# Three stacked blocks on one core: the experts' low weight parts all on VectorE, the embeddings' product at the routing, the last gate's weights as blocks of the experts' pipeline

## The chip, the cores and the metric

The kernel runs on one core of one Trainium2 chip. The metric is the time of one execution on the device in microseconds; the time before is the median of three runs. All sums below are made on one profiled execution of the kernel before.

## The reference, cut to what matters

Three blocks follow each other on 512 tokens of 1024 numbers: an mLSTM and sparse attention block, a gated recurrent and gMLP block, and a block with 32 experts. The change touches only the end of the third. There a router picks 4 of 32 experts for each token, each expert is a gated product with 1024 x 2048 weights and a second one with 1024 x 1024, and the rows are added up per token. Then come a layer norm, a gate of the embeddings `p` and a last layer norm:

```python
def third_block(x, p, ...):
    ...
    x = layer_norm(DEEPNORM_ALPHA_3 * x + mix, ln1_g[i], ln1_b[i])
    ffn = moe(x, router_w[i], router_b[i], w_gate_up[i], b_gate_up[i], w_down[i], b_down[i])
    x = layer_norm(DEEPNORM_ALPHA_3 * x + ffn, ln2_g[i], ln2_b[i])
    gate = jax.nn.sigmoid((x @ ple_gate_w[i] + ple_gate_b[i]).astype(jnp.float32)).astype(x.dtype)
    ple = p[i] @ ple_proj[i]
    x = layer_norm(DEEPNORM_ALPHA_3 * x + gate * ple, ln3_g[i], ln3_b[i])
```

The product `ple` needs nothing of `x`, so it may be made at any time. All numbers are float32.

## The kernel before, in words

A float32 product is made of three products of shorter floats (`mm3`): the weights are split into a high part `hi`, which ScalarE (ACT) writes as a rounded copy, and a low part `lo`, which is the difference of the weights and `hi`. So each block of weights goes through three rings of tiles of 1 MB each: `wl` (where it lands), `wh` (high) and `wo` (low). In the experts' stage `wl` has 5 tiles and `wh` and `wo` have 4 each.

The experts' stage is `run`. Its list `steps` has 384 entries of one 1 MB block each: expert i has 8 `wide` steps (`w_gate_up`, 12 matmuls each), and behind them stand 4 `narrow` steps (`w_down`, 12 matmuls each) of expert i-1. In each step `load` issues the transfer of a block 7 steps ahead on SyncE's queue (SP), `halve` makes the two parts of the block 3 steps ahead, and `step` runs the matmuls. In `halve` ACT makes `hi`, and `lo` is subtracted by VectorE (DVE) in three steps of four and by GpSimd (POOL) in every fourth (`n % 4 == 1`). POOL also gathers the tokens of the expert after next (`fetch`, tile `xg`) and adds the finished rows to `yd` in memory (`add_rows`). DVE also makes the gated activation (`glu`) and the low parts of the tokens (`turn`). Each engine runs its instructions in the order in which they are written; within the experts' steps that is the program's order (`manual_schedule`), elsewhere a scheduler sets it.

Ahead of the experts' steps the routing works token tile by token tile (`route`, `places`, `biased`): layer norm, transposes, logits, the choice of four, the positions. Behind them `ple` and `ended` do the end: `project` makes the product of the embeddings with `ple_proj` (8 transposes, 48 matmuls into `pa`), four blocks of `ple_gate_w` are loaded and split, the rows of `yd` come back as `zs`, are normed, turned and multiplied with the gate's weights (`pz`), and are normed once more.

In PSUM the tag `gemm` has 4 banks, and `run` calls `layout` so that `aux` and `hold` have 2 each.

Of the kernel before, what the change touches and what calls it, by code (L numbers as in the profile page):

```python
# [19 lines left out]
P = 128  # L20
S = 512
D = 1024
# [8 lines left out]

class Env:
    def __init__(self, ctx, tc):
        self.tc, self.nc = tc, tc.nc
        nc = self.nc
        self.n = 0
# [4 lines left out]
        self.psx = ctx.enter_context(ExitStack())  # L41
        self.layout(gemm=4, aux=3, hold=1)
        self.dram = ctx.enter_context(tc.tile_pool(name="dr", bufs=1, space=bass.MemoryType.DRAM))
        self.ident = self.cst.tile([P, P], F32, name="ident")
        make_identity(nc, self.ident)
        self.half = self.cst.tile([P, 1], F32, name="half")
        nc.gpsimd.memset(self.half, -0.5)
        self.rings = {"wl": [(self.wl, "wl")] * 3, "wh": [(self.wh, "wh")] * 2, "wo": [(self.wo, "wo")] * 2}
        self.at = dict.fromkeys(self.rings, 0)
        self.banks, self.owner = [], {}  # L50
# [20 lines left out]
    def name(self, s):  # L71
        self.n += 1
        return f"{s}_{self.n}"

    def layout(self, **banks):

        self.BANKS = banks
        self.psx.close()
        self.psp = self.psx.enter_context(self.tc.tile_pool(name=self.name("ps"), bufs=4, space=bass.MemoryType.PSUM))

# [1266 lines left out]
class Moe:  # L1347
# [58 lines left out]

    def project(self, pj, lp):

        e, nc, a = self.e, self.e.nc, self.a
        parts = lp.tile([P, 2, 2, 4, P], F32R, tag="xp", name="parts", bufs=3).rearrange("p g a k n -> p (g a) (k n)")  # L1410
        hi, lo = parts[:, :2, :], parts[:, 2:, :]
        for t in range(NT):
            pt = self.wp.tile([P, 512], F32, tag="g", name=e.name("pt"))[:, :256]
            nc.sync.dma_start(pt, a["p_3"][0, 0, t * P:(t + 1) * P, :])
            pz = e.ps("pz").rearrange("p (a b) -> p a b", a=4)
            for j in range(2):
                nc.tensor.transpose(pz[:, j, :], pt[:, j * P:(j + 1) * P], e.ident)
            ts = slice(t * P, (t + 1) * P)
            e.split(hi[:, :, ts], lo[:, :, ts], pz[:, :2, :])

        def got(t, c, n, pz):
            nc.scalar.activation(pj[t][:, c:c + n], pz, AF.Copy)
        e.gemm_tok([(hi, lo)], 2, a["ple_proj_3"][0], 0, D, got)
# [117 lines left out]
    def run(self, out):  # L1541
        e, nc, tc, wp = self.e, self.e.nc, self.e.tc, self.wp
        e.layout(gemm=4, aux=2, hold=2)
        ph = ExitStack()
# [64 lines left out]
        for i in range(N_EXP + 1):  # L1609
# [6 lines left out]
        lands, tiles = [], []  # L1616

        def load(n):
            if n < len(steps):
                land = e.ring("wl")  # L1620
                nc.sync.dma_start(land.rearrange("p a b -> p (a b)"), steps[n][3])
# [18 lines left out]
        with tc.manual_schedule():  # L1640
# [23 lines left out]
        ph.close()  # L1664
        self.ple(out)

# [110 lines left out]

    def ple(self, out):

        with self.e.tc.tile_pool(name=self.e.name("pl"), bufs=1) as lp:  # L1780
            self.ended(out, lp)

    def ended(self, out, lp):
        e, nc, a, wp = self.e, self.e.nc, self.a, self.wp
        wg, w, rows = a["ple_gate_w_3"][0], {}, []

        def row_pair(land, nm):
# [3 lines left out]
        land = e.res.tile([P, NT, D], F32, tag="res", name="rows")  # L1791
        own = lp.tile([P, 6, D], F32, name="own")
        zs, pj = [own[:, t, :] for t in range(NT)], [own[:, 4, :], own[:, 5, :]] + [land[:, 2 + i, :] for i in range(2)]
# [9 lines left out]
        def first(t):  # L1803
            z = zs[t]
            nc.sync.dma_start(z, self.yd[t * P:(t + 1) * P, :])
            if t == 0:
                for k0 in (0, 4):
                    w[512, k0] = e.wblock(wg, k0, 4, 512, 512, z[:, 0:1], ("wl", "wl") if k0 else ("wh", "wo"))
            if t == 1:
                nc.vector.tensor_copy(land[:, 0:2, 0], z[:, 0:2])  # L1810
                row_pair(land, "ln3")
            norm(z, 0)
# [3 lines left out]
        def gate(t):  # L1816
            z = zs[t]
            for c in (0, 512):
# [8 lines left out]
                nc.scalar.activation(g, pz, AF.Sigmoid)  # L1827
                nc.vector.tensor_tensor(g, g, pj[t][:, cs], op=ALU.mult)
                nc.vector.scalar_tensor_tensor(z[:, cs], z[:, cs], ALPHA, g, op0=ALU.mult, op1=ALU.add)
# [6 lines left out]
        for t in range(NT):  # L1836
# [3 lines left out]
            if t:  # L1840
                last(t - 1)
        last(NT - 1)


# [48 lines left out]
```

## Time and profile before

| | us |
|---|---|
| time before, median of 3 runs (3303.92 to 3329.73) | 3324.47 |
| the profiled execution's own time | 3329.63 |
| its span | 3327.9 |
| stretch before the routing of the last tiles, 0 to 1881 | 1881 |
| routing, 1881 to 1944 | 63 |
| experts' steps, 1944 to 3244 | 1300 |
| end, 3244 to 3328 | 84 |

Times in the rows are counted from the start of the span. "PE" is TensorE, "PEld" its loading of weights. A matmul's end is modelled, so two starts that follow each other tell its cost better than its duration. What stands in brackets behind a row is how long the engine was idle before it, and what ended that.

### The profile page before, as it was taken

The numbers are of one execution on the slowest core, as the hardware profiler recorded it, in microseconds if no ns is written. First come the engines' busy times: TensorE is split into PE (matmuls) and PEld (weight loads), VectorE is DVE, ScalarE is ACT, GpSimd is POOL, SyncE is SP. The second block draws the span as 40 slices with busy tenths as digits, with TensorE's granted clock in tenths as the row PEclk, the third lists the DMA queues.
The fourth block names the chain that finished last, engine by engine and source line by source line (L and its number), as shares of the span: only waits on it lengthen the run. The fifth ranks groups of instructions, "written<-read, shape, count | busy, mean of one in ns | idle before, by whom it ended". The sixth has DMA issues, their size and how long they took to land. (4 is left out here: it accounts for less than half of the span.)

```text
span 3327.9 us, 36769 instructions
## 1 busy us (share of the span) xinstructions
PE 3157.5 (95%) x14603; PEld 2392.9 (72%) x14603; DVE 2246.5 (68%) x2365; ACT 1518.3 (46%) x1547; POOL 905.0 (27%) x333
## 2 busy tenths in 40 slices
PE   7999999999999999999999989999999999989987
PEld 6776877878777787888778766666666666666666
DVE  5853687444726533722345769899898898899876
ACT  5353333323635223122313246666666666666652
POOL 2310011101000001100000125555555555555531
PEclk9997999999999999999999979999999999999999
DMA  4212465333121423222223269899998999898882
GB/s 141 77 39 81 145 206 197 108 114 102 51 76 51 124 89 134 94 89 89 94 93 105 107 244 342 326 335 333 341 340 323 329 337 331 325 330 325 323 301 98
DMA packets 180207, 639.50 MB, mean 192 GB/s; under 512 B 25656, under 2 KB 33184, under 8 KB 130810
## 3 DMA queue, kind: packets, MB, share of 16 engines
q1 hardware_dynamic: 172858, 611.89, 51.0%
q0 software_dynamic: 7168, 25.17, 3.2%
q8 instruction: 117, 1.92, 0.2%
q14 instruction: 64, 0.52, 0.0%
HBM read 616.01 MB, written 21.01 MB: 191 GB/s over the span
## 5 line engine op out<-in xcount | busy, mean ns | idle before, releaser
L1629 DVE TENSOR_TENSOR wo<-wl,wh 128x2048 fp32r<-128x2048 f32 x288 | 945.6, 3309 | 129.1 <-ACT wh L1627 125.3
L1627 ACT ACTIVATE wh<-wl 128x2048 fp32r<-128x2048 f32 x384 | 725.2, 1912 | 164.0 <-PE pgu L167 104.3
L99 DVE TENSOR_TENSOR wo<-wl,wh 128x2048 fp32r<-128x2048 f32 (+2 forms) x147 | 320.9, 2186 | 543.3 <-ACT wh L98 534.6
L1629 POOL TENSOR_TENSOR wo<-wl,wh 128x2048 fp32r<-128x2048 f32 x96 | 486.8, 5071 | 531.0 <-ACT wh L1627 521.3
L167 PE MATMUL pf<-ah,wo 128*128 128x512 f32 (+1 forms) x1520 | 564.2, 371 | 1.2 <-DVE wo L99 1.2
L166 PE MATMUL pf<-ah,wh 128*128 128x512 f32 (+1 forms) x1520 | 563.3, 371 | 0.6 <-ACT wh L98 0.6
L98 ACT ACTIVATE wh<-wl 128x2048 fp32r<-128x2048 f32 (+2 forms) x153 | 277.5, 1817 | 621.1 <-PE pf L168 320.9
L168 PE MATMUL pf<-al,wh 128*128 128x512 f32 (+1 forms) x1520 | 560.0, 369 | 0.0
L168 PE MATMUL pgu<-wo,xe 128*96 128x512 f32 x1024 | 413.9, 404 | 47.9 <-DVE wo L1629 47.9
L166 PE MATMUL pgu<-wh,xe 128*96 128x512 f32 x1024 | 416.9, 407 | 0.0
L167 PE MATMUL pgu<-wh,xe 128*96 128x512 f32 x1024 | 412.1, 402 | 0.0
L166 PEld LDWEIGHTS pf<-ah,wh 128*128 128x128 f32 x1520 | 287.4, 189 | 58.8 <-ACT cy L728 6.9
L168 PEld LDWEIGHTS pf<-al,wh 128*128 128x128 f32 x1520 | 286.5, 189 | 51.7 <-issue 3.7
L167 PEld LDWEIGHTS pf<-ah,wo 128*128 128x128 f32 x1520 | 287.2, 189 | 49.5 <-DVE wo L99 1.4
L168 PEld LDWEIGHTS pgu<-wo,xe 128*96 128x96 f32 x1024 | 170.3, 166 | 129.8 <-DVE wo L1629 57.2
L168 PE MATMUL pd<-wo,h 128*96 128x512 f32 x512 | 207.1, 405 | 37.4 <-DVE wo L1629 36.7
L167 PEld LDWEIGHTS pgu<-wh,xe 128*96 128x96 f32 x1024 | 170.0, 166 | 68.1 <-issue 1.2
L166 PEld LDWEIGHTS pgu<-wh,xe 128*96 128x96 f32 x1024 | 170.1, 166 | 66.3 <-issue 0.9
L167 PE MATMUL pd<-wh,h 128*96 128x512 f32 x512 | 205.3, 401 | 4.1 <-DVE h L114 4.1
L166 PE MATMUL pd<-wh,h 128*96 128x512 f32 x512 | 205.6, 402 | 2.0 <-ACT h L113 1.1
L168 PEld LDWEIGHTS pd<-wo,h 128*96 128x96 f32 x512 | 84.7, 165 | 87.2 <-DVE wo L1629 51.1
L1561 POOL DMA_INDIRECT xg<-x3d,src x32 | 126.4, 3948 | 72.8 <-DVE src L1559 54.7
(476 smaller groups left out, 4615.8 us busy)
## 6 DMA issues: line engine op xcount, KB each, us to landing
wl<-w_gate_up SPq DMA_DIRECT2D x256, 1024.0 KB
wl<-w_down SPq DMA_DIRECT2D x138, 1024.0 KB
wl<-w_in SPq DMA_DIRECT2D x54, 1024.0 KB
wl<-w_ada SPq DMA_DIRECT2D x24, 1024.0 KB
wl<-w_up SPq DMA_DIRECT2D x20, 1024.0 KB
wl<-w_ffn_in SPq DMA_DIRECT2D x20, 1024.0 KB
wl<-w_out SPq DMA_DIRECT2D x12, 1024.0 KB
wl<-w_ffn_out SPq DMA_DIRECT2D x10, 1024.0 KB
```

The costliest lines, as they stand in the source:

```text
L98: nc.scalar.activation(hi[:, :nk, :n], land[:, :nk, :n], AF.Copy)
L99: (eng or nc.vector).tensor_tensor(lo[:, :nk, :n], land[:, :nk, :n], hi[:, :nk, :n].bitcast(F32), op=ALU.subtract)
L166: mm(out, st[0], mv[0], start=first, stop=False)
L167: mm(out, st[1], mv[0], start=False, stop=False)
L168: mm(out, st[0], mv[1], start=False, stop=last)
L1561: nc.gpsimd.indirect_dma_start(out=rows[i], out_offset=None, in_=self.xd, in_offset=bass.IndirectOffsetOnAxis(ap=src[:, :1], axis=0))
L1627: nc.scalar.activation(hi, land, AF.Copy)
L1629: eng.tensor_tensor(lo, land, hi.bitcast(F32), op=ALU.subtract)
```

## The change

- `halve`: DVE subtracts `lo` in all steps; POOL subtracts none.
- `project` is called at the start of `run`, so it stands in the program at the routing. Its result is kept in a tile `pj` of 16 KB per partition, its split embeddings take a tile of the `wh` ring, and the 48 matmuls, 8 transposes and 6 transfers move with it.
- The four blocks of `ple_gate_w` are four more entries of `steps`, without matmuls: they are loaded and halved like an expert's, and their tiles are kept for the end.
- `layout` is gone: `aux` has 3 banks and `hold` 1 throughout, and an expert's second accumulator `pd` comes from `aux`. The rows of the last two layer norms are both loaded into `wl`, `y` has one buffer, and the rows `zs` have a pool of their own.

```diff
-        self.layout(gemm=4, aux=3, hold=1)
+    BANKS = {"gemm": 4, "aux": 3, "hold": 1}
...
     def run(self, out):
-        e.layout(gemm=4, aux=2, hold=2)
+        self.project()
...
-                acc[i] = [e.ps("pd", "hold")[:CAP, :] for _ in range(2)]
+                acc[i] = [e.ps("pd", tag)[:CAP, :] for tag in ("hold", "aux")]
...
-            y = wp.tile([P, D], F32, tag="y", name=e.name("y"))[:CAP, :]
+            y = wp.tile([P, D], F32, tag="y", name=e.name("y"), bufs=1)[:CAP, :]
...
+        wg = self.a["ple_gate_w_3"][0]
+        steps += [(None, c, k0, wg[k0 * P:(k0 + 4) * P, c:c + 512].rearrange("(k p) n -> p k n", p=P)) for c in (0, 512) for k0 in (0, 4)]
...
                 nc.scalar.activation(hi, land, AF.Copy)
-                eng = nc.gpsimd if n % 4 == 1 else nc.vector
-                eng.tensor_tensor(lo, land, hi.bitcast(F32), op=ALU.subtract)
+                nc.vector.tensor_tensor(lo, land, hi.bitcast(F32), op=ALU.subtract)
...
                 halve(n + ahead)
+                if step is None:
+                    w[i, k] = tiles.pop(0)
+                    continue
...
-        self.ple(out)
+        self.ple(out, w)
...
-        self.project(pj, lp)
-        row_pair(e.ring("wl").rearrange("p (g i) n -> p g (i n)", g=2), "ln2")
-        for k0 in (0, 4):
-            w[0, k0] = e.wblock(wg, k0, 4, 0, 512)
...
-            if t == 0:
-                for k0 in (0, 4):
-                    w[512, k0] = e.wblock(wg, k0, 4, 512, 512, z[:, 0:1], ("wl", "wl") if k0 else ("wh", "wo"))
```

How the order changes is shown at three places. The first is SP's queue at the routing, before the change: `w_gate_up` is an expert's weights, `x3d` and `yd` are the tokens written to memory, of which the last `x3d` waits for the last tile's layer norm.

```order
L1621 DMA wl_13236<-w_gate_up 128x2048
L1621 DMA wl_13238<-w_gate_up 128x2048
L1429 DMA x3d<-xres 128x1024 x2
L1776 DMA yd<-xres 128x1024
L1429 DMA x3d<-xres 128x1024
L1621 DMA wl_13240<-w_gate_up 128x2048
L1776 DMA yd<-xres 128x1024
L1621 DMA wl_13242<-w_gate_up 128x2048
L1621 DMA wl_13244<-w_gate_up 128x2048
L1621 DMA wl_13250<-w_gate_up 128x2048
L1429 DMA x3d<-xres 128x1024
```

The same queue after the change, where `ple_proj` and `p` are the embeddings' weights and rows.

```order
L88 DMA wl_13167<-ple_proj 128x2x512
L88 DMA wl_13205<-ple_proj 128x2x512
L1425 DMA x3d<-xres 128x1024 x2
L1776 DMA yd<-xres 128x1024
L1425 DMA x3d<-xres 128x1024
L1776 DMA yd<-xres 128x1024
L1410 DMA pt_13139<-p 128x256
L1410 DMA pt_13146<-p 128x256
L1425 DMA x3d<-xres 128x1024
L1619 DMA wl_13338<-w_gate_up 128x2048
L1410 DMA pt_13153<-p 128x256
L1410 DMA pt_13160<-p 128x256
```

Six loads of experts' weights stood ahead of the last `x3d`; now none does, and the second of them stands behind the last rows of `p`.

The second place is DVE between an expert's gated activation `g` and the low parts of `h`, before the change.

```order
L1534 SCALAR_TENSOR_TENSOR g_20032<-u_20038,g_20032 96x512
L1629 TENSOR_TENSOR wo_20045<-wl_19942,wh_20044 128x2048
L1629 TENSOR_TENSOR wo_20065<-wl_19968,wh_20064 128x2048
L1629 TENSOR_TENSOR wo_20101<-wl_20012,wh_20100 128x2048
L114 SCALAR_TENSOR_TENSOR h_20120<-pt_20121,h_20120 128x384
L114 SCALAR_TENSOR_TENSOR h_20128<-pt_20129,h_20128 128x384
```

The same after the change.

```order
L1530 SCALAR_TENSOR_TENSOR g_20134<-u_20140,g_20134 96x512
L1626 TENSOR_TENSOR wo_20147<-wl_20044,wh_20146 128x2048
L1626 TENSOR_TENSOR wo_20167<-wl_20070,wh_20166 128x2048
L1626 TENSOR_TENSOR wo_20185<-wl_20096,wh_20184 128x2048
L1626 TENSOR_TENSOR wo_20203<-wl_20114,wh_20202 128x2048
L109 SCALAR_TENSOR_TENSOR h_20222<-pt_20223,h_20222 128x384
L109 SCALAR_TENSOR_TENSOR h_20230<-pt_20231,h_20230 128x384
```

All four subtractions stand on DVE where three did; TensorE's order in the experts' steps is the same before and after.

The third place is SP's queue at the end, before the change, from the last expert's weights on.

```order
L1621 DMA wl_22312<-w_down 128x2048
L1414 DMA pt_22466<-p 128x256
L1414 DMA pt_22473<-p 128x256
L93 DMA wl_22494<-ple_proj 128x2x512
L93 DMA wl_22532<-ple_proj 128x2x512
L1789 DMA wl_22570<-ln_g 128x1024
L1789 DMA wl_22570<-ln_b 128x1024
L93 DMA wl_22573<-ple_gate_w 128x4x512
L93 DMA wl_22579<-ple_gate_w 128x4x512
L1414 DMA pt_22480<-p 128x256
L1414 DMA pt_22487<-p 128x256
L1805 DMA own<-yd 128x1024 x3
```

The same after the change.

```order
L1619 DMA wl_22414<-w_down 128x2048
L1619 DMA wl_22434<-ple_gate_w 128x4x512
L1619 DMA wl_22452<-ple_gate_w 128x4x512
L1619 DMA wl_22470<-ple_gate_w 128x4x512
L1619 DMA wl_22508<-ple_gate_w 128x4x512
L1788 DMA wl_22586<-ln_g 128x1024
L1788 DMA wl_22586<-ln_b 128x1024
L1788 DMA wl_22589<-ln_g 128x1024
L1788 DMA wl_22589<-ln_b 128x1024
L1800 DMA z_22595<-yd 128x1024
```

The embeddings' six transfers are gone from the end, and all four gate blocks stand ahead of the read of `yd`, where two stood behind it.

## Rows read from the trace of the kernel before

**Rows 1.** The page: the span, and each engine's busy time, share and instructions.

```profile
span 3327.9 us, 36769 instructions
...
PE 3157.5 (95%) x14603; PEld 2392.9 (72%) x14603; DVE 2246.5 (68%) x2365; ACT 1518.3 (46%) x1547; POOL 905.0 (27%) x333
```

**Rows 2.** Busy time by stretch: PE, PEld, DVE, ACT, POOL; granted clock, DMA share, GB/s.

```profile
1881.00:1944.00 63.00, 50.35 (x218) 38.56 (x216) 39.54 (x92) 14.45 (x24) 9.55 (x5) 0.76 0.44 168
1944.00:3244.00 1300.00, 1204.15 (x5360) 839.89 (x5359) 1155.18 (x738) 841.91 (x640) 709.11 (x156) 0.97 0.89 326
...
3259.00:3328.00 69.00, 52.75 (x232) 41.77 (x232) 47.97 (x75) 14.03 (x19) 10.99 (x7) 0.92 0.20 74
```

**Rows 3.** Waits, 1944 to 3244: engine, line, waited for: us, times, longest.

```profile
PE pgu L168 <- DVE wo L1629: 47.9, 20, 2.7
PE pd L168 <- DVE wo L1629: 36.7, 31, 3.3
ACT wh L1627 <- DMA wl<-w_gate_up: 19.1, 11, 2.9
ACT wh L1627 <- DMA wl<-w_down: 10.6, 10, 2.2
```

**Rows 4.** Groups by line, 1944 to 3244: busy us, mean ns | idle before.

```profile
L1629 DVE TENSOR_TENSOR wo<-wl,wh 128x2048 fp32r<-128x2048 f32 x285 | 938.7, 3320 | 129.0 <-ACT wh L1627 125.3
...
L1629 POOL TENSOR_TENSOR wo<-wl,wh 128x2048 fp32r<-128x2048 f32 x95 | 482.3, 5077 | 523.2 <-ACT wh L1627 513.5 <-PE pgu L167 7.1 <-PE pgu L168 2.7
...
L1561 POOL DMA_INDIRECT xg<-x3d,src x30 | 124.3, 4142 | 52.3 <-DVE src L1559 50.5 <-issue 0.9
```

**Rows 5.** Timeline, POOL and DVE, 2598 to 2636: start us, duration us, instruction.

```profile
2598.34 4.62 POOL L1629 TENSOR_TENSOR wo<-wl,wh 128x2048 fp32r<-128x2048 f32 x1 [2.87 <-ACT wh L1627]
...
2600.45 4.66 DVE L1629 TENSOR_TENSOR wo<-wl,wh 128x2048 fp32r<-128x2048 f32 x1 [2.51 <-ACT wh L1627]
...
2608.81 4.49 DVE L1629 TENSOR_TENSOR wo<-wl,wh 128x2048 fp32r<-128x2048 f32 x2
...
2630.01 4.48 DVE L1629 TENSOR_TENSOR wo<-wl,wh 128x2048 fp32r<-128x2048 f32 x2
...
2630.37 4.94 POOL L1561 DMA_INDIRECT xg<-x3d,src  x1 [2.81 <-DVE src L1559]
```

**Rows 6.** As Rows 2: the fullest 10 us, and the fullest whole 100 us.

```profile
2510.00:2520.00 10.00, 10.00 (x49) 7.10 (x48) 5.97 (x5) 6.51 (x5) 5.58 (x2) 0.96 1.01 384
...
2300.00:2400.00 100.00, 93.38 (x427) 65.72 (x426) 92.39 (x62) 65.53 (x49) 57.73 (x14) 0.98 0.93 340
```

**Rows 7.** Timeline of the routing, 1905 to 1923: POOL, DVE and PE.

```profile
1905.04 4.54 POOL L1629 TENSOR_TENSOR wo<-wl,wh 128x2048 fp32r<-128x2048 f32 x1 [7.76 <-ACT wh L1627]
...
1905.38 4.36 DVE L1448 TENSOR_TENSOR hot<-ie,fi 128x128 f32<-128x128 f32 x1
...
1910.72 0.63 PE L1455 MATMUL pp<-mask,upper 128*128 128x32 f32 x2 [3.40 <-DVE mask L1450]
...
1919.63 2.28 DVE L1629 TENSOR_TENSOR wo<-wl,wh 128x2048 fp32r<-128x2048 f32 x1
...
1922.63 1.97 PE L1434 MATMUL pt<-ident,xres 128*128 128x128 f32 x8 [6.00 <-DVE xres L270]
```

**Rows 8.** Timeline of the end, 3243 to 3265: PE and POOL.

```profile
3243.56 0.39 PE L168 MATMUL pd<-wo,h 128*96 128x512 f32 x1
...
3244.95 1.56 POOL L1747 DMA_INDIRECT yd<-y,dst  x1 [12.74 <-ACT parts L110]
...
3257.24 0.39 PE L167 MATMUL pa<-wh,parts 128*128 128x512 f32 x1
3257.47 0.40 PE L168 MATMUL pa<-wo,parts 128*128 128x512 f32 x1
3258.97 1.29 PE L1515 MATMUL pt<-ident,own 128*128 128x128 f32 x8 [1.10 <-DVE own L270]
...
3264.32 0.50 PE L166 MATMUL pz<-wh,xp 128*128 128x512 f32 x1 [2.84 <-ACT wh L98]
```

More of the change, by code (lines that the diff above doesn't have):

```diff
@@ L35, in __init__ @@
         nc = self.nc
-        self.n = 0
         self.cst = ctx.enter_context(tc.tile_pool(name="cst", bufs=1))
@@ L40, in __init__ @@
         self.wo = ctx.enter_context(tc.tile_pool(name="wo", bufs=2))
-        self.psx = ctx.enter_context(ExitStack())
-        self.layout(gemm=4, aux=3, hold=1)
+        self.psp = ctx.enter_context(tc.tile_pool(name="ps", bufs=4, space=bass.MemoryType.PSUM))
         self.dram = ctx.enter_context(tc.tile_pool(name="dr", bufs=1, space=bass.MemoryType.DRAM))
@@ L47, in __init__ @@
         nc.gpsimd.memset(self.half, -0.5)
+        self.n = 0
         self.rings = {"wl": [(self.wl, "wl")] * 3, "wh": [(self.wh, "wh")] * 2, "wo": [(self.wo, "wo")] * 2}
@@ L73, in name @@
         return f"{s}_{self.n}"
[L75 to L79, printed above, removed]
     def ps(self, s, tag="aux"):
@@ L1405, in __init__, with project @@
         nc.vector.tensor_copy(self.sel, pick)
-    def project(self, pj, lp):
+    def project(self):
         e, nc, a = self.e, self.e.nc, self.a
-        parts = lp.tile([P, 2, 2, 4, P], F32R, tag="xp", name="parts", bufs=3).rearrange("p g a k n -> p (g a) (k n)")
+        self.pj = self.wp.tile([P, NT, D], F32, tag="pj", name=e.name("pj"), bufs=1)
+        parts = e.ring("wh", F32R)
         hi, lo = parts[:, :2, :], parts[:, 2:, :]
@@ L1421, in got @@
         def got(t, c, n, pz):
-            nc.scalar.activation(pj[t][:, c:c + n], pz, AF.Copy)
+            nc.scalar.activation(self.pj[:, t, c:c + n], pz, AF.Copy)
         e.gemm_tok([(hi, lo)], 2, a["ple_proj_3"][0], 0, D, got)
@@ L1615, in run @@
                 steps += [(narrow, i - 1, j, w[j * 256:(j + 1) * 256, :].rearrange("(p i) n -> p (i n)", i=2)) for j in range(4)]
-        lands, tiles = [], []
+        wg = self.a["ple_gate_w_3"][0]
+        steps += [(None, c, k0, wg[k0 * P:(k0 + 4) * P, c:c + 512].rearrange("(k p) n -> p k n", p=P)) for c in (0, 512) for k0 in (0, 4)]
+        lands, tiles, w = [], [], {}
         def load(n):
@@ L1620, in load @@
                 land = e.ring("wl")
-                nc.sync.dma_start(land.rearrange("p a b -> p (a b)"), steps[n][3])
+                nc.sync.dma_start(land.rearrange("p a b -> p (a b)") if steps[n][0] else land, steps[n][3])
                 lands.append(land)
@@ L1776, in biased, with ple @@
         nc.sync.dma_start(self.yd[t * P:(t + 1) * P, :], x[:, t, :])
[L1778 to L1783, printed above, removed]
+    def ple(self, out, w=None):
         e, nc, a, wp = self.e, self.e.nc, self.a, self.wp
-        wg, w, rows = a["ple_gate_w_3"][0], {}, []
-        def row_pair(land, nm):
+        if w is None:
+            self.project()
+            w = {(c, k0): e.wblock(a["ple_gate_w_3"][0], k0, 4, c, 512) for c in (0, 512) for k0 in (0, 4)}
+        rows = []
+        for nm in ("ln2", "ln3"):
+            land = e.ring("wl").rearrange("p (g i) n -> p g (i n)", g=2)
             for i, c in enumerate("gb"):
@@ L1790, in row_pair @@
                 rows.append(land[:, i, :])
-        land = e.res.tile([P, NT, D], F32, tag="res", name="rows")
-        own = lp.tile([P, 6, D], F32, name="own")
-        zs, pj = [own[:, t, :] for t in range(NT)], [own[:, 4, :], own[:, 5, :]] + [land[:, 2 + i, :] for i in range(2)]
-        self.project(pj, lp)
-        row_pair(e.ring("wl").rearrange("p (g i) n -> p g (i n)", g=2), "ln2")
-        for k0 in (0, 4):
-            w[0, k0] = e.wblock(wg, k0, 4, 0, 512)
+        ph = ExitStack()
+        lp = ph.enter_context(e.tc.tile_pool(name=e.name("pl"), bufs=1))
+        zs = [lp.tile([P, D], F32, name=e.name("z")) for _ in range(NT)]
         xs = {}
@@ L1805, in first @@
             nc.sync.dma_start(z, self.yd[t * P:(t + 1) * P, :])
-            if t == 0:
-                for k0 in (0, 4):
-                    w[512, k0] = e.wblock(wg, k0, 4, 512, 512, z[:, 0:1], ("wl", "wl") if k0 else ("wh", "wo"))
-            if t == 1:
-                nc.vector.tensor_copy(land[:, 0:2, 0], z[:, 0:2])
-                row_pair(land, "ln3")
             norm(z, 0)
@@ L1827, in gate @@
                 nc.scalar.activation(g, pz, AF.Sigmoid)
-                nc.vector.tensor_tensor(g, g, pj[t][:, cs], op=ALU.mult)
+                nc.vector.tensor_tensor(g, g, self.pj[:, t, cs], op=ALU.mult)
                 nc.vector.scalar_tensor_tensor(z[:, cs], z[:, cs], ALPHA, g, op0=ALU.mult, op1=ALU.add)
@@ L1842, in ended @@
         last(NT - 1)
+        ph.close()
 def rel_hot():
```

## The prediction

> **What bounds the kernel now.** I read the page first, then the stretches, then inside the longest stretch that the change touches the waits, the groups by line and the timeline. The page says that PE is busy 95% of a span of 3327.9 us and DVE 68% [rows 1]: PE is the engine to watch, and its missing time is little and has to be looked for stage by stage. Up to the routing nothing is changed. The experts' stretch takes 1300 us [rows 2]. There PE is busy for 1204 us, so it stands idle for 96, at a granted clock of 0.97, a mean of stretches at 2.4 and at 1.2 GHz: 0.97 x 1204 = 1168 us is what PE would need without idle time and at the full clock. DVE is busy 1155 of the 1300 us, the DMA engines 0.89 of them at 326 GB/s.
>
> What ends PE's idle time there is one thing: a low part `wo` that DVE delivers late, 47.9 us before `wide` and 36.7 us before `narrow` matmuls, together 84.6 of the 96 us; ACT's waits for landing weights are 19.1 + 10.6 = 29.7 us [rows 3]. So the stage is held up by the low parts, not by the transfers.
>
> Why DVE is late is read from its durations. The subtraction has a mean of 3320 ns on DVE over 285 of them, and 5077 ns on POOL over 95 [rows 4]. The timeline shows that the mean is a mixture. Where POOL subtracts nothing, two in a row take 4.49 and 4.48 us, 2.25 each; the one that starts at 2600.45, while POOL subtracts from 2598.34 to 2602.96, takes 4.66 [rows 5]. It ends at 2605.11, 2.15 us after POOL: it has waited for POOL to finish and then run at its own speed. The two engines take turns at these subtractions. A block given to POOL costs DVE up to 4.6 us of standing, twice what making it itself would cost.
>
> **The low parts all on DVE.** Removed: 96 subtractions on POOL. Added: 96 on DVE at 2.25 us, 216 us of work. Removed with them: what DVE stands behind POOL, 285 x (3.32 - 2.25) = 305 us [rows 4, 5]. What else DVE does in the stretch is 1155 - 939 = 216 us [rows 2, 4]. So DVE comes to 384 x 2.25 + 216 = 1080 us of work, 75 less than before, and a low part is ready 2.25 us after its turn instead of up to 4.66 on DVE and 5.08 on POOL. The waits of PE for `wo`, 84.6 us, should go; I take -85 for the stage, which gives 1215 us. Nothing is taken for the clock that would rise as the waits go, and nothing for a wait that comes instead; they are the two bounds. Below, PE without idle time at the full clock: 1168 us, -132. Above, the transfers: 1300 us at 326 GB/s move 424 MB, with the gate's 4.2 MB 428 MB. The fullest 100 us moved 340 GB/s, the fullest 10 us 384 at a share of 1.01 [rows 6]. At 384 the stream needs 1115 us and bounds nothing; if 340 were all that it can hold, it needs 1259 us, -41. I take the value between because 340 was reached while the loads still waited for tiles that the subtractions free.
>
> The Trainium skill (DMA: Bandwidth & Descriptors, "Where 436 GB/s comes from") says that memory feeds one core at about 358 GB/s. By that estimate 428 MB need 1196 us and the stage could gain 104 us at most, which would rule out the lower bound; the 384 GB/s of the 10 us window speak against it, and the sum goes without it.
>
> POOL keeps the gathers and the additions into `yd`. A gather now runs beside more subtractions; one at 2630.37 beside two of them took 4.94 us, and the mean is 4.14 [rows 4, 5]. It is issued in the third step of one expert and used in the fifth of the next, 14 steps of 1300/384 = 3.4 us later, 47 us. That cover hides it. The four gate steps hold no matmul, so they lie beside the last experts' steps; the accumulator from `aux` and the single `y` are written once per expert, some 40 us apart, and cost nothing while an expert takes longer than the addition's few us.
>
> **The product at the routing.** PE gets 48 matmuls and 8 transposes there. At the full clock a matmul costs 0.23 us (two starts at 3257.24 and 3257.47 [rows 8]), so 11 us; the routing ran at a mean clock of 0.76 [rows 2], and at 1.2 GHz they cost 22. Transposes, their splits and the second pair of `p` rows, which can only be fetched when the first pair has been turned, add some 3 us. They stand in PE's order between the last tile's logits and the experts' first step, where PE waits little, so I count them as path: +14 to +25.
>
> Against that, DVE's low parts for the first experts leave the routing's chain. POOL's subtraction at 1905.04 made DVE's `hot` take 4.36 us, on which PE then waited 3.40; another on DVE at 1919.63 (2.28 us) lies in the layer norm for which PE waits 6.00 [rows 7]. Both waits shorten, by 3.4 and about 2, and PE, which idles less, should run more of the 63 us at 2.4 GHz: of the (1 - 0.76) x 50 = 12 us that the low clock costs there I take a third. Together -9 (0 to -14). SP's queue is moved past too: the experts' first blocks, six of which were issued ahead of the last `x3d`, now follow it. At 384 GB/s a block takes 2.7 us, so the first four need 11 us, which the 14 us of the product hide. Net for the routing: +8, from 0 to +25.
>
> **The end.** The 48 matmuls go from here, but they cost nothing here: between the last `pd` at 3243.56 and the first transposes at 3258.97 the path is y, the addition to `yd` (3244.95), the read of `yd` and the layer norm; the matmuls filled PE's wait [rows 8]. Its end stays. What goes is the 2.84 us for which the gate's product waited for its split weights. What comes is that PE, idle for some 14 us, starts the gate at 1.2 GHz; the last stretch already has a mean clock of 0.92 [rows 2], 0.08 x 53 = 4 us. I take -1, between -4 and +4.
>
> **Sum.** -85 + 8 - 1 = -78 us against the profiled execution's 3329.63 us, 3251.6. That execution lies 5.2 us above the median of the three runs; I take this off: **3246 us**.
>
> **The rivals.** (a) The transfers become the bound at 340 GB/s: -41 + 8 - 1 = -34, about 3290 us. For it: the DMA share is 0.89 now and would have to reach 0.95 in the forecast; against it: 384 GB/s over 10 us and only 29.7 us of waits for weights. (b) The clock comes back as well and nothing new waits: -132 + 8 - 1 = -125, 3199. For it: the clock is 0.97 only because PE idles; against it: the stream would have to hold 428 MB / 1168 us = 366 GB/s throughout. (c) Slower: DVE's 3.32 us are its own price, not POOL's doing, as they would be if the incoming weights slowed it. Then it needs 384 x 3.32 + 216 = 1491 us, +191, about 3523. It decides from (1300 - 216) / 384 = 2.82 us per subtraction on. Against it: the pairs at 2.25 us in the midst of the stage, with transfers under way. (d) The change moves the work and gains nothing: the gain in the stage stays under 20 us because DVE, busy 1080 of 1280, is late in its bursts (six operations of `glu`, then four subtractions in a row), and the routing's +25 eats it: about 3329. For it: DVE stays the fullest engine but PE. Against it: the four narrow steps, 48 matmuls of 0.23 us, are 11 us long, and the burst's four subtractions 9.
>
> **How the numbers follow.** Forecast 0.60, (a) 0.16, (b) 0.13, (c) 0.04, (d) 0.07. The forecast's own range is 3225 to 3275, from the routing's bounds and half of the way to (a). The range that should hold 8 in 10 reaches to (b) and (a): 3196 to 3302. Three runs of before spread over 26 us, 0.8%, so under 1% cannot be told from no change. Faster by over 1% (under 3291): the forecast, (b) and two thirds of (a), 0.84. Within 1%: the rest of (a) and most of (d), 0.10. Slower: (c) and a little of (d), 0.06.
>
> **What would show it.** Right: DVE's subtractions have a mean of 2.2 to 2.4 us and none over 4; PE's waits for `wo` in the experts' steps fall from 84.6 us to under 20; the stage takes some 1215 us and its DMA share passes 0.93; the experts' first step starts 0 to 25 us later than before, measured from the last tile's logits; the end from the last `pd` keeps its 84 us within 5. Wrong: ACT's waits for landing weights rise from 29.7 us towards 100 (then the transfers bound it), subtractions stay over 3 us with POOL idle, or PE waits between the product's last matmul and the experts' first by more than 10 us.

## The result and the profile after

The changed kernel took 3201.42 us, the median of four runs (3197.41 to 3208.69), beside 3322.51 us for the kernel before (3303.92 to 3329.73) on the same chip: a ratio of 0.9646, 95% interval 0.9602 to 0.969. The profiled execution took 3197.41 us; its span is 132.2 us shorter than that of before.

The page of the changed kernel, the lines that answer to [rows 1]:

```profile
span 3195.7 us, 36723 instructions
...
PE 3113.9 (97%) x14603; PEld 2378.5 (74%) x14603; DVE 2146.3 (67%) x2458; ACT 1520.4 (48%) x1547; POOL 393.8 (12%) x237
```

DVE has 93 instructions more than before and is busy 100 us less; POOL has lost 511 of its 905 us. Where the time went is read from the stretches, in the columns of [rows 2]: the routing, the experts' stage, one full 100 us of it, and the end from the first transposes on.

```profile
1881.00:1946.00 65.00, 57.98 (x262) 45.08 (x263) 37.98 (x97) 20.35 (x37) 4.30 (x4) 0.85 0.47 175
1946.00:3116.00 1170.00, 1165.60 (x5364) 827.17 (x5362) 1060.20 (x834) 846.52 (x639) 203.28 (x62) 1.00 0.97 364
...
2346.00:2446.00 100.00, 100.00 (x464) 70.97 (x463) 90.88 (x74) 71.84 (x53) 16.80 (x5) 1.00 1.00 374
...
3131.00:3196.00 65.00, 51.20 (x227) 41.16 (x225) 43.67 (x72) 10.32 (x17) 10.99 (x7) 0.89 0.09 34
```

The stage is 130 us shorter, on PE in two parts: idle time fell from 96 us to 4.4, which is 91 us, and the busy time of the same matmuls from 1204 to 1166 at a granted clock of 1.00 instead of 0.97, which is 39. In the full 100 us PE never stands, and the DMA engines move 374 GB/s at a share of 1.00. The waits of the stage that answer to [rows 3] are these; no wait of PE for a `wo` is left, nor one of ACT for landing weights.

```profile
PE pgu L1576 <- DVE g L1523: 1.9, 1, 1.9
...
PE pgu L162 <- DVE xe L106: 1.1, 1, 1.1
...
PE pd L162 <- DVE h L109: 0.7, 1, 0.7
```

The groups by line of the stage, as [rows 4], and a stretch of the timeline in which two subtractions lie beside a gather, as [rows 5]:

```profile
L1626 DVE TENSOR_TENSOR wo<-wl,wh 128x2048 fp32r<-128x2048 f32 x384 | 867.9, 2289 | 108.8 <-ACT wh L1625 102.9
...
L1557 POOL DMA_INDIRECT xg<-x3d,src x31 | 108.9, 3514 | 288.5 <-issue 119.2 <-DMA yd<-y,dst 119.1 <-PE pgu L162 24.9
```

```profile
2499.36 5.72 POOL L1557 DMA_INDIRECT xg<-x3d,src  x1 [8.51 <-issue]
2499.79 4.48 DVE L1626 TENSOR_TENSOR wo<-wl,wh 128x2048 fp32r<-128x2048 f32 x2
```

All 384 subtractions take 2.29 us, none is stretched, beside a gather no more than elsewhere (4.48 us for two). A gather may take longer beside them, but its mean fell from 4.14 to 3.51 us.

PE's timeline at the routing, and PE, POOL and SP's queue at the end (answering to [rows 7] and [rows 8]):

```profile
1913.04 1.78 PE L1430 MATMUL pt<-ident,xres 128*128 128x128 f32 x8 [4.33 <-DVE xres L265]
...
1921.49 0.80 PE L161 MATMUL pa<-wh,wh 128*128 128x512 f32 x1 [0.99 <-ACT wh L93]
...
1936.42 0.40 PE L163 MATMUL pa<-wo,wh 128*128 128x512 f32 x1
...
1946.49 0.74 PE L161 MATMUL pgu<-wh,xe 128*96 128x512 f32 x1
...
3115.91 0.40 PE L163 MATMUL pd<-wo,h 128*96 128x512 f32 x1
...
3117.31 1.54 POOL L1747 DMA_INDIRECT yd<-y,dst  x1 [11.38 <-ACT y L1600]
3122.68 1.75 SPq L1800 DMA_DIRECT2D z<-yd  x4
...
3130.35 1.94 PE L1511 MATMUL pt<-ident,z 128*128 128x128 f32 x8 [14.04 <-DVE z L265]
```

The product occupies PE from 1921.49 to 1936.82, and the first wide matmul starts at 1946.49, 2.3 us later in the span than before (1944.22). From the last `pd` the end takes 3195.7 - 3115.9 = 79.8 us instead of 84.4; PE now stands for 14.0 us before the first transposes. The three places make up the whole difference: -130 + 2.3 - 4.6 = -132; the 2.3 holds 2 us by which this execution was ahead before the routing's last tile.

### The profile page after: what moved, and what is told of

It is laid out like the page before. It is cut to its first block, busy times and chain, and to the rows that moved or that the text cites. A ratio compares the mean times of both kernels' runs of the same rounds, so it can differ in the third digit from the quotient of the medians.

```text
span 3195.7 us, 36723 instructions
## 1 busy us (share of the span) xinstructions
PE 3113.9 (97%) x14603; PEld 2378.5 (74%) x14603; DVE 2146.3 (67%) x2458; ACT 1520.4 (48%) x1547; POOL 393.8 (12%) x237
## 5 line engine op out<-in xcount | busy, mean ns | idle before, releaser
L1626 DVE TENSOR_TENSOR wo<-wl,wh 128x2048 fp32r<-128x2048 f32 x388 | 877.0, 2289 | 114.1 <-ACT wh L1625 108.2
L1625 ACT ACTIVATE wh<-wl 128x2048 fp32r<-128x2048 f32 x388 | 733.1, 1913 | 150.9 <-PE pgu L162 143.4
L94 DVE TENSOR_TENSOR wo<-wl,wh 128x2048 fp32r<-128x2048 f32 (+2 forms) x144 | 314.1, 2185 | 533.6 <-ACT wh L93 533.6
L161 PE MATMUL pgu<-wh,xe 128*96 128x512 f32 x1024 | 410.4, 401 | 0.0
L162 PE MATMUL pgu<-wh,xe 128*96 128x512 f32 x1024 | 406.0, 397 | 1.1 <-DVE xe L106 1.1
L163 PE MATMUL pgu<-wo,xe 128*96 128x512 f32 x1024 | 404.2, 395 | 0.0
L162 PEld LDWEIGHTS pgu<-wh,xe 128*96 128x96 f32 x1024 | 166.1, 162 | 67.8 <-DVE xe L106 1.7
L161 PEld LDWEIGHTS pgu<-wh,xe 128*96 128x96 f32 x1024 | 166.5, 163 | 66.9 <-ACT xe L105 0.3
L161 PE MATMUL pd<-wh,h 128*96 128x512 f32 x512 | 202.3, 395 | 0.2 <-ACT h L108 0.2
L162 PE MATMUL pd<-wh,h 128*96 128x512 f32 x512 | 201.8, 394 | 0.7 <-DVE h L109 0.7
L1747 POOL DMA_INDIRECT yd<-y,dst x32 | 96.1, 3003 | 691.7 <-ACT y L1600 691.7
L1557 POOL DMA_INDIRECT xg<-x3d,src x32 | 110.1, 3441 | 308.8 <-issue 119.2
L161 PE MATMUL pa<-wh,ah 128*128 128x512 f32 x352 | 142.5, 405 | 0.0
```

The source lines that it names most:

```text
L94: (eng or nc.vector).tensor_tensor(lo[:, :nk, :n], land[:, :nk, :n], hi[:, :nk, :n].bitcast(F32), op=ALU.subtract)
L161: mm(out, st[0], mv[0], start=first, stop=False)
L162: mm(out, st[1], mv[0], start=False, stop=False)
L163: mm(out, st[0], mv[1], start=False, stop=last)
L1557: nc.gpsimd.indirect_dma_start(out=rows[i], out_offset=None, in_=self.xd, in_offset=bass.IndirectOffsetOnAxis(ap=src[:, :1], axis=0))
L1626: nc.vector.tensor_tensor(lo, land, hi.bitcast(F32), op=ALU.subtract)
```

## The experiments

The question was where the 130 us of the stage come from and what the low parts and the two moved pieces (the product, the gate's blocks) carry of them, then what the turns of DVE and POOL hang on, and what binds next. The table gives for each kernel's profiled execution the time from the last logits matmul `pl` to the first wide matmul, from there to the last `pd` (the stage), and from there to the span's end, all from starts in the timeline; then the median, and its ratio to the runs of the kernel before on the same chip.

| kernel | pl to stage | stage | end | median us | ratio (95%) |
|---|---|---|---|---|---|
| before | 15.7 | 1299.3 | 84.4 | 3322.5 | 1 |
| after_again | 27.7 | 1167.9 | 80.4 | 3199.4 | 0.9631 (0.961 to 0.9651) |
| dve_only | 15.7 | 1163.6 | 86.2 | 3190.9 | 0.9597 (0.9576 to 0.9617) |
| moves_only | 29.8 | 1261.0 | 82.4 | 3300.2 | 0.9929 (0.9904 to 0.9954) |
| before_banks | 15.0 | 1282.2 | 80.8 | 3314.7 | 0.9982 (0.9966 to 0.9997) |
| late_product | 15.0 | 1161.3 | 86.3 | 3191.6 | 0.9602 (0.9583 to 0.9622) |
| late_product2 | 15.0 | 1162.7 | 82.9 | 3187.8 | 0.959 (0.9574 to 0.9605) |
| pool_reads | 17.4 | 1362.4 | 85.5 | 3391.2 | 1.0199 (1.0175 to 1.0222) |
| pool_copies | 15.7 | 1213.5 | 86.3 | 3244.3 | 0.9753 (0.9733 to 0.9773) |
| pool_writes | 15.9 | 1164.1 | 86.0 | 3192.5 | 0.9608 (0.9585 to 0.963) |
| two_products | 27.8 | 1144.6 | 79.6 | 3177.7 (one run) | |
| one_product | 25.4 | 1121.6 | 80.3 | 3152.9 (one run) | |

**after_again.** The changed kernel, unedited, on the chip of the next three.

> The changed kernel once more, as the yardstick for the three kernels beside it on the same chip. Expected 3197 to 3209 us, the range of its four times so far, and a stage from the first wide matmul to the last pd of 1169 us within 5.

It came as expected: 3199.36 us, stage 1167.9.

**dve_only.** The kernel before, with one edit in `halve`:

```diff
-                eng = nc.gpsimd if n % 4 == 1 else nc.vector
-                eng.tensor_tensor(lo, land, hi.bitcast(F32), op=ALU.subtract)
+                nc.vector.tensor_tensor(lo, land, hi.bitcast(F32), op=ALU.subtract)
```

> The kernel before, with every low part subtracted on VectorE and nothing moved. Theory (the engines take turns, and the whole gain of the stage is POOL's absence): the stage falls from 1299 to 1170 us within 10, subtractions all at 2.3 us, the routing is some 8 us shorter because the low parts leave its chain, the end keeps its 84 us; in all 3328 - 130 - 8, about 3190 us, a little faster than the changed kernel. Rival (the gate's blocks in the pipeline and the routing's new order are needed for a part of it): the stage stays over 1200 us and the time over 3225.

The theory held: 3190.88 us, and the stage alone, in the columns of [rows 2], and its subtractions:

```profile
1941.00:3105.00 1164.00, 1159.78 (x5358) 825.61 (x5357) 1055.77 (x832) 841.73 (x638) 203.00 (x61) 0.99 0.97 364
```

```profile
L1628 DVE TENSOR_TENSOR wo<-wl,wh 128x2048 fp32r<-128x2048 f32 x380 | 858.7, 2288 | 99.6 <-ACT wh L1627 92.9 <-PE pgu L168 0.9
```

The one edit gives the whole gain of the stage, 136 us; the two moved pieces add nothing to it (with the product at the routing the stage is 4 to 6 us longer; why is open). All of its runs (3186.65 to 3194.21) lie under all of the changed kernel's beside it (3197.8 to 3205.32): the moves cost some 8 us. Of the expected 8 us at the routing 6.3 came, ahead of the last `pl`: from the third tile's logits to the last tile's transposes it takes 15.1 us where before takes 21.4. In the span its last `pl` is only 3 us earlier (1925.5 against 1928.6), because this execution reached the third tile 3.3 us later; from `pl` on it has the 15.7 us of before.

**moves_only.** The changed kernel with that edit undone.

> The changed kernel with every fourth low part back on POOL; the product stays at the routing and the gate's blocks in the pipeline. Theory: the stage is back at 1300 us within 15, subtractions beside POOL at 4.6 us, the routing some 12 us longer than before, the end 5 us shorter; about 3335 us, between 3320 and 3350. Rival (the moves carry part of the gain): under 3300 us.

Both were off: 3300.22 us, and the stage came to 1261, not 1300. The stage and what is left of PE's waits for `wo` in it:

```profile
1957.00:3218.00 1261.00, 1195.80 (x5361) 832.84 (x5361) 1144.00 (x738) 845.09 (x639) 720.30 (x158) 0.98 0.92 339
```

```profile
PE pd L163 <- DVE wo L1627: 44.4, 31, 1.6
PE pgu L163 <- DVE wo L1627: 6.9, 3, 2.3
```

The waits of `narrow` have not fallen (44.4 us after 36.7), those of `wide` have, from 47.9 us [rows 3] to 6.9. The timelines of one expert, of the kernel before and then of moves_only, show how the same order of instructions on each engine comes to differ. (A row with x2 holds two subtractions; its second one starts at 2500.20 in the first and at 2510.09 in the second.)

```profile
2498.00 8.99 DVE L1629 TENSOR_TENSOR wo<-wl,wh 128x2048 fp32r<-128x2048 f32 x2
2500.16 4.67 POOL L1629 TENSOR_TENSOR wo<-wl,wh 128x2048 fp32r<-128x2048 f32 x1 [1.71 <-ACT wh L1627]
...
2507.04 0.47 PE L168 MATMUL pgu<-wo,xe 128*96 128x512 f32 x1 [2.41 <-DVE wo L1629]
```

```profile
2507.89 4.47 DVE L1627 TENSOR_TENSOR wo<-wl,wh 128x2048 fp32r<-128x2048 f32 x2
2510.08 6.77 POOL L1627 TENSOR_TENSOR wo<-wl,wh 128x2048 fp32r<-128x2048 f32 x1 [1.73 <-ACT wh L1625]
```

In both, POOL's subtraction and the second of DVE's pair start almost together: DVE's 33 ns behind POOL's in the first, 11 ns behind in the second. Before, POOL has the first turn: it takes 4.67 us, and DVE's ends 2.2 us after it, so the next low part is late and PE waits 2.41. In moves_only DVE has the first turn: its pair takes 4.47, and POOL's takes 6.77, 2.2 us of standing and 4.6 of its own, and PE does not wait there. All such pairs of before, moves_only and before_banks (the next run), 77 that start within 0.25 us of each other, go the same way: where DVE's start stands at most 25 ns behind POOL's, DVE has the first turn (38 of 38), and from 25 ns on POOL has it (39 of 39). POOL has it 22, 3 and 14 times in the three kernels, and every one of the 20, 3 and 11 waits of `wide` follows such a pair within 0.1 us. Without POOL's subtractions there is nothing to win in this way, which is why the moves add nothing in the changed kernel.

**before_banks.** The kernel before with the changed kernel's PSUM banks in the stage, as the suspect for this shift.

```diff
-        e.layout(gemm=4, aux=2, hold=2)
+        e.layout(gemm=4, aux=3, hold=1)
...
-                acc[i] = [e.ps("pd", "hold")[:CAP, :] for _ in range(2)]
+                acc[i] = [e.ps("pd", tag)[:CAP, :] for tag in ("hold", "aux")]
```

> The kernel before with one edit that the change brings along: in the experts' stage three PSUM banks for aux and one for hold, a pd accumulator from each. POOL keeps its subtractions. It is to tell why moves_only, with POOL's subtractions, came to a stage of 1261 us and not to 1299. Theory (the layout shifts by some 10 ns which engine gets its turn first where both start together, at the third step of an expert, and so when the fifth step's low part is there): the stage falls to 1261 within 15, the waits in the fifth wide step from 53 us to under 15, the time to 3270 to 3300 us. Rival (something else of the moves does it): stage and time stay as before, 1299 and 3323 us, within 10.

Neither: 3314.72 us and a stage of 1282, and of the waits of `wide` (53 us if counted from the starts, 47.9 in [rows 3]) about half is left.

```profile
PE pd L168 <- DVE wo L1629: 43.9, 31, 3.3
PE pgu L168 <- DVE wo L1629: 26.1, 11, 2.4
```

So with the banks 11 of these waits are left in place of 20. Each count is of one profiled execution, and the times differ by 0.2% alone, so the banks' part is not sure; which of the other moves does the rest stays open.

**late_product.** The changed kernel with the product moved back behind the last `pd`; its weights are landed and split in free `wl` tiles, its rows in `g` and `u` tiles, and the gate's blocks stay in the pipeline. The core of the edit (`late` holds the old loops, with both halves of the weights ready):

```diff
     def run(self, out):
-        self.project()
...
+                if n == len(steps) - 8:
+                    land, ps = self.ready()
                 load(n + loaded)
                 halve(n + ahead)
+                if n == len(steps) - 5:
+                    proj = self.parted(land)
...
+        if ps is not None:
+            self.late(lp, ps, proj)
```

> The changed kernel with the embeddings' product back at the end, in PE's wait between the last pd and the gate's first transposes, its weights loaded and halved with the gate's blocks. Theory (the product lies on the routing's path, and at the end it costs nothing and keeps PE at work): the first wide matmul comes 12 us earlier after the last tile's logits, the end keeps its 80 us or loses some 3 more; 12 to 15 us less than the changed kernel, about 3186 us. Rival 1 (the product fills a wait that stands there anyway, for gathered rows or first blocks): no difference, within 4 us of the changed kernel. Rival 2 (at the end the product makes the first gate matmul late, since its weights land behind the gate's): the end is over 88 us and the gain is gone.

The theory held at the routing: 15.0 us from `pl` to the stage in place of 27.7, so the product costs 12 to 13 us there. Its end took 86.3 us, 6 more than the changed kernel's, and the time is 3191.6 us; the weights that rival 2 feared for are not the reason, since the product was done 6 us before the first transposes. POOL's addition and the read of `yd` in the timeline, of late_product and then of after_again:

```profile
3105.33 0.33 SPq L1830 DMA_DIRECT2D wl<-ln_g  x1
3105.70 0.43 SPq L1830 DMA_DIRECT2D wl<-ln_b  x1
3106.19 2.59 POOL L1789 DMA_INDIRECT yd<-y,dst  x1 [14.12 <-ACT parts L105]
3107.53 0.33 SPq L1830 DMA_DIRECT2D wl<-ln_g  x1
3107.91 0.42 SPq L1830 DMA_DIRECT2D wl<-ln_b  x1
3116.88 1.76 SPq L1844 DMA_DIRECT2D z<-yd  x4
```

```profile
3118.64 1.54 POOL L1747 DMA_INDIRECT yd<-y,dst  x1 [11.38 <-ACT y L1600]
3124.97 1.75 SPq L1800 DMA_DIRECT2D z<-yd  x4
```

From the addition to the read it is 10.7 us in the one and 6.3 in the other; in the one, four rows of 512 KB each were issued around the addition, in the other none within 4 us of it. POOL's own instruction is longer there too (2.59 us after 1.54).

**late_product2.** As late_product, with `parted` behind `ends(i)`, and the second pair of rows behind the reads of `yd`:

```diff
             nc.sync.dma_start(z, self.yd[t * P:(t + 1) * P, :])
+            if t == 1:
+                row_pair("ln3", z)
```

> late_product with two orders mended at the end. There the addition into yd and the read back took 10.7 us from the one's start to the other's issue, against 6.3 in the changed kernel, while four rows of the layer norms (2 MB) were on their way, and y began 1.1 us after the last pd because ACT split the product's weights first. Now ACT writes y before it splits them, and the second pair of rows is loaded behind the reads of yd. Theory (the rows' transfers and that split cost the end its 6 us): the end falls from 86 to 80 us or a little less, stage and routing stay as in late_product, 1161 and 15 us; about 3185 us, 12 to 15 less than the changed kernel. Rival (PE, busy with the product, is itself late for the first gate matmuls): the end stays over 84 us and the time at 3190.

The end fell to 82.9 us, a little over half of what was expected, and the time to 3187.83 us: the lowest of the kernels that compute the whole product, with an interval (0.9574 to 0.9605) under the changed kernel's (0.961 to 0.9651). It is not told apart from dve_only's (0.9576 to 0.9617): the one edit in `halve` is as fast, within the noise, as any of them.

```profile
3103.33 1.57 POOL L1789 DMA_INDIRECT yd<-y,dst  x1 [12.86 <-ACT y L1638]
3103.65 0.33 SPq L1833 DMA_DIRECT2D wl<-ln_g  x1
3104.03 0.43 SPq L1833 DMA_DIRECT2D wl<-ln_b  x1
3111.98 1.76 SPq L1848 DMA_DIRECT2D z<-yd  x4
```

From the addition to the read it is 8.65 us now, with one pair of rows issued behind the addition. The other traces bear it out: 10.2 to 10.8 us in the four kernels with four rows around the addition (late_product and the three built on it below), 8.65 with two in this one, 5.4 to 7.5 in the eight with none within 4 us. The rival holds for a little: the first transposes follow the product's last matmul at once, 5.6 us after the layer norm's start (3115.50 to 3121.08), where the changed kernel needs 4.3 (3126.04 to 3130.35).

**pool_reads.** To separate DVE's standing from POOL's own late blocks: late_product, in which POOL works on a tile of its own, `junk`, that nobody waits for.

```diff
                 nc.vector.tensor_tensor(lo, land, hi.bitcast(F32), op=ALU.subtract)
+                if n % 4 == 1 and steps[n][0]:
+                    h32 = hi.rearrange("p a b -> p (a b)").bitcast(F32)
+                    nc.gpsimd.tensor_tensor(junk, h32, h32, op=ALU.subtract)
```

> The kernel late_product (stage 1161 us, 3192 us), in which POOL besides, in every fourth step of the experts, subtracts a high part from itself into a tile that nothing reads; VectorE still makes every low part, and nobody waits for POOL's result. Theory (the two engines take turns whenever both run such a subtraction, whoever needs the result): VectorE's subtractions beside it take 4.6 us and more, 80 to 100 of 383 of them; the stage grows by 60 to 140 us; the time is between 3250 and 3330 us. Rival (PE waited because the blocks that POOL made were themselves late, or because both engines worked on the same ring of tiles for the same consumer): the subtractions stay at 2.3 us or their stretching costs nothing; the stage stays at 1161 within 10, the time at 3192 within 10.

The theory held, and its price was too low: the stage grew by 201 us, 2.1 for each of POOL's 95 subtractions, and the time to 3391.19 us. The stage, and its groups in the greater part of it:

```profile
1946.00:3308.00 1362.00, 1230.40 (x5356) 842.07 (x5356) 1342.42 (x833) 843.83 (x638) 726.81 (x156) 0.96 0.86 312
```

```profile
L1665 DVE TENSOR_TENSOR wo<-wl,wh 128x2048 fp32r<-128x2048 f32 x325 | 974.3, 3042 | 13.6 <-ACT wh L1664 11.3
...
L1669 POOL TENSOR_TENSOR junk<-wh 128x2048 f32<-128x2048 f32 x82 | 423.7, 5168 | 400.7 <-ACT wh L1664 396.2 <-DVE wo L1665 4.1
```

DVE is busy 1342 of 1362 us: with all 384 low parts and the standing besides, it has become the bound. Here no block of POOL's can be late, and DVE's mean is 3.04 us.

**pool_copies and pool_writes.** The same with an instruction of one input, and with one of none:

```diff
-                    nc.gpsimd.tensor_tensor(junk, h32, h32, op=ALU.subtract)
+                    nc.gpsimd.tensor_copy(junk, h32)
```

```diff
-                    nc.gpsimd.tensor_tensor(junk, h32, h32, op=ALU.subtract)
+                    nc.gpsimd.memset(junk, 0.0)
```

> As pool_reads, but POOL copies the high part into the tile that nothing reads: one input where the subtraction has two. Theory (any reading of SBUF by POOL takes turns with a subtraction of two SBUF inputs on VectorE): the subtractions beside it stretch to 3 us and more, the stage is over 1200 and the time over 3230 us. Rival (it takes two inputs on both engines): subtractions stay at 2.3 us, the stage at 1161 within 10, the time at 3192 within 10.

> As pool_reads, but POOL fills that tile with zeros in place of the subtraction: it writes as many elements and reads nothing. Theory (it is the two inputs that the engines take turns for): VectorE's subtractions stay at 2.3 us, the stage at 1161 within 10, the time at 3192 within 10. Rival (any POOL instruction on as much data holds VectorE up): subtractions beside it stretch to 3 us and more, the stage is over 1200 and the time over 3230 us.

In both the theory held on the subtractions: the copy stretches them, the fill does not. The copy's stage is 1213.5 us and its time 3244.34; the fill's are 1164.1 and 3192.5, those of late_product. Their groups by line, the copy's first:

```profile
L1665 DVE TENSOR_TENSOR wo<-wl,wh 128x2048 fp32r<-128x2048 f32 x367 | 962.9, 2668 | 15.5 <-ACT wh L1664 11.6
L1669 POOL COPY junk<-wh 128x2048 f32<-128x2048 f32 x92 | 274.7, 2986 | 552.8 <-ACT wh L1664 552.3
```

```profile
L1665 DVE TENSOR_TENSOR wo<-wl,wh 128x2048 fp32r<-128x2048 f32 x383 | 865.3, 2288 | 104.7 <-ACT wh L1664 98.7
L1668 POOL MEMSET junk<- 128x2048 f32 x94 | 185.6, 1975 | 2.0
```

The fill was tested beside subtractions, not only between them: 67 of the 383 lie beside one for more than 0.3 us, and none takes over 2.30. So it is POOL's reading. This is what the Trainium skill (SBUF — State Buffer, "Who interferes with whom") states: a DVE instruction with two inputs in SBUF contends with a POOL instruction that reads SBUF, and not with one that only writes; the traces agree: among POOL's copies the mean is 2.67 us, a mixture again, of 289 subtractions at 2.28 and 94 at 3.85, and among its fills it is 2.29. It adds that the order of issue decides who stands; the 77 pairs of moves_only, before and before_banks agree, with the turn changing at 25 ns between their starts.

**two_products.** What binds next? The changed kernel, with the second matmul of `mm3` left out in `wide`: the product of the rows' low part with the weights' high part is not computed.

> The changed kernel without the second of the three products in the wide matmuls (the rows' low part times the weights' high part is left out), so that PE needs only 112/144 of its 1168 us in the stage, 908, and whatever comes next binds. Theory 1 (the transfers are not yet the limit at the changed kernel's 364 GB/s): the stage falls to VectorE's 384 x 2.29 + 216 = 1095 us or to the transfers at 384 GB/s, 1115 us; between 1095 and 1130, at 378 to 391 GB/s. Theory 2 (364 to 370 GB/s is all that the transfers hold, and the changed kernel stands at that limit): the stage stays between 1155 and 1170 us.

Between the two: 1144.6 us, at 373 GB/s and a share of 0.99. The stage and its waits:

```profile
1952.00:3096.00 1144.00, 994.93 (x4334) 668.26 (x4334) 1050.14 (x834) 838.83 (x638) 189.67 (x62) 0.96 0.99 373
```

```profile
PE pd L163 <- DVE wo L1628: 84.8, 81, 1.6
ACT wh L1627 <- DMA wl<-w_gate_up: 84.0, 57, 2.9
ACT wh L1627 <- DMA wl<-w_down: 58.4, 60, 3.5
```

A third of the wide matmuls less gives 25 us, and there are waits for both transfers and DVE, so this run alone does not tell which of them holds it.

**one_product.** It leaves both out: of `wide` only the first product is computed, and the wide blocks' low parts are not made.

> The changed kernel with the wide matmuls cut to the first of their three products, and the low parts of the wide blocks left out with them: PE needs 80/144 of 1168 us in the stage, 649, and VectorE 128 x 2.29 + 216 = 509. What is left is the stream of weights, all of which still lands and passes through ACT, 384 x 1.92 = 737 us and some 100 of other work. Theory 1 (the transfers held two_products at 1145 us): the stage stays at 1145 within 10, 374 GB/s. Theory 2 (there it was VectorE, 1095 us of work in bursts): the stage falls under 1125 us, to the transfers at 384 GB/s or more.

Theory 2: 1121.6 us.

```profile
1949.00:3071.00 1122.00, 859.78 (x3314) 550.02 (x3312) 502.16 (x581) 834.15 (x639) 78.56 (x62) 0.81 1.00 381
```

With DVE busy 502 of 1122 us and the DMA engines all of it, this is the stream alone: 381 GB/s over the whole stage. So the transfers were not all that held two_products at 1145. That the rest was DVE in its bursts is likely by PE's 84.8 us of waits for `wo` there, but not shown: this run takes matmuls from PE as well as low parts from DVE, and each of the two kernels ran once.

## Why the prediction was right, and what was mis-sized

**The mechanism was right.** DVE and POOL took turns, the low parts were late by that, and PE's waits for `wo` fell from 84.6 us to none where under 20 was forecast. DVE's mean is 2.29 us with none stretched (2.2 to 2.4, none over 4). dve_only shows that this edit alone carries the stage's gain, and pool_reads that DVE's standing is enough for the harm, whoever needs POOL's result. Rivals (c) and (d) are out: 2.29 us is DVE's price in the midst of the transfers, and its bursts leave no wait.

**The stage's term was mis-sized: -85 forecast, -130 measured** (1299.3 to 1169.4; 1167.9 in the second execution). The step that failed is "nothing is taken for the clock that would rise as the waits go". The clock rose, from 0.97 to 1.00, and PE's busy time fell by 39 us beside the 91 us of idle time. Those 39 are most of the 45 us between -85 and -130; the other 6 us are idle time, 91 where 85 was counted. The lower bound of the term, -132, was nearly reached. In pool_reads, where the waits are back, it is 0.96 again. What happened is rival (b), 3199 us against 3201, to which 0.13 was given. What spoke against it was that the stream would have to hold 366 GB/s throughout. It held 364 over the stage and 374 in a full 100 us, and one_product shows 381 over a whole stage with the DMA engines at a share of 1.00. The 340 GB/s of the fullest 100 us before was thus not a limit of the transfers; the loads stood behind tiles that were late in coming free (SP's queue waited 995 of the 1300 us for low parts of DVE and POOL), as the prediction had noted and then counted at half. Rival (a) falls with it. The 10 us at 384 GB/s of [rows 6] are the fullest of 2500 to 2710 alone; 2710 to 2720 moved 406.

The sentence on the Trainium skill's 358 GB/s per core (DMA: Bandwidth & Descriptors, "Where 436 GB/s comes from") would have limited the gain to 104 us; 130 were measured, so the measurement decides against it here. The Trainium skill's HBM Reference ("Specifications (TRN2)") has that a core streaming alone goes well above that share; 381 GB/s of this lone core agrees.

**The routing: +8 forecast, +2.3 measured** (+5.1 in the second execution, whose first wide matmul starts at 1949.3), both within 0 to +25. These starts in the span also carry what ran before. Counted from the third tile's logits, of before and then of the changed kernel, the stage starts 4.3 us later than before, and 4.4 in the second execution:

```profile
1901.20 0.97 PE L1438 MATMUL pl<-rw,xt 128*128 128x32 f32 x8
```

```profile
1899.19 0.97 PE L1434 MATMUL pl<-rw,xt 128*128 128x32 f32 x8
```

Its two halves can be told apart. The product's price was +14 to +25; between the last logits and the stage it is 27.7 us with it and 15.0 or 15.7 without (late_product, dve_only), so 12 to 13. On PE the 48 matmuls and what lies between them take 15.3 us, where 11 at the full clock and 22 at half were the bounds. The gain in the chain was put at -9 (0 to -14): from the third tile's logits to the last tile's transposes it is 13.9 us (1899.19 to 1913.04) where it was 21.4 (1901.20 to 1922.63 [rows 7]), so -7.6. What brings it is not POOL's absence alone, as the prediction had it: dve_only has 15.1 us, but moves_only, with POOL's subtractions, has 13.9 too. There, as in the changed kernel, the experts' first blocks come behind the routing, and no subtraction of theirs starts before the last logits. PE's wait for the layer norm fell with that move alone, to 4.33 us from 6.00 [rows 7] (it is 6.00 in dve_only); the wait for `hot` is gone in all three. The wait named as a sign of error, between the product's last matmul and the first wide one, did not come from the blocks' transfers: those 10 us are biases, places and the turn of the first rows, and in the timeline PE stands for 0.37 and 0.93 us in them.

**The end: -1 forecast, -4.6 and -4.0 measured**, just outside the bounds of 4. The 2.84 us of waiting for split weights went, as counted; but before_banks, whose end is not edited, lacks that wait too and takes 80.8 us, and dve_only, not edited there either, 86.2. How much of the 4 us is the change's is therefore not shown. The 4 us put down for a gate that starts at the lower clock did not come: from the first transposes on, PE is busy 51.2 us, not more than the 52.8 of before [rows 2], at a clock of 0.89 against 0.92. That the 48 matmuls were free at the end is confirmed by late_product, where they fit between the last `pd` and the first transposes; what its end lost lies between the addition and the read of `yd`. Where that wait is shorter, in late_product2, they cost 1.3 us.

**The sum.** -85 + 8 - 1 was forecast and -130 + 2.3 - 4.6 measured; 45 of the 54 us between them are the stage's term. The measured 3201 us lie within the range of 3196 to 3302, near its lower end, and there only because that range reached to rival (b); the forecast's own range, 3225 to 3275, missed them.

## What to carry to other kernels

Before giving POOL a share of DVE's elementwise work, look for a mixture of durations in the group's mean: where a subtraction takes 2.25 us alone and 4.66 beside POOL, the share costs more than it takes off, while fills and gathers do no such harm. When waits of one or two us are scattered over a stage that PE bounds, count the stage's gain with the clock that they hold down, and read the transfers' limit from the share at 1.00, not from the GB/s of a stage that still waits for tiles (374 and 381 GB/s at 1.00 here, 326 before). A piece that fills a wait is best left there: the product cost 0 to 1.3 us at the end and 12 at the routing, but what is issued beside it must not meet the transfer that the wait is for.

## What the runs showed of the hardware

Three things stand in no term of the prediction. Two subtractions, one on DVE and one on POOL, that start almost together are served one after the other; whether DVE's start was less or more than 25 ns behind decided the turn in all 77 pairs, and with it 47.9 or 6.9 us of PE's waits over a stage. A copy on POOL, which reads one input, already stretches DVE's subtractions, to a mean of 2.67 us, while a fill of the same size leaves them at 2.29. And from the addition into `yd` to its read back it took 5.4 to 7.5 us with no rows issued within 4 us of it (8 kernels), 8.65 with two of 512 KB (one kernel) and 10.2 to 10.8 with four (4 kernels).
